# A hybrid attention and MLP layer on one core: 26 identity transposes at the start, and every engine's order drawn anew from refitted durations

## The chip, the cores and the metric

The kernel runs on one core of a Trainium2 chip. Five engines work through lists of their own: TensorE (PE in the profile; its weight loads are PEld), VectorE (DVE), ScalarE (ACT), GpSimd (POOL) and SyncE (SP), which only issues DMAs. An engine takes its list strictly in order; an instruction whose operand is not there holds up all behind it. The metric is the device time of one execution in us, the median of several runs.

## The reference

One layer of a decoder, 1024 tokens of width 1024. Cut to what is computed:

```python
h = rms_norm(x, g_mix_norm)
z = h @ w_in                               # q, 6 x k/v, gates, 3 x conv parts
k_cmp = rms_norm(compress(kc, ...)); v_cmp = compress(vc, ...)   # 63 blocks of 32 tokens, 2-layer MLP
attn_out = nsa_attention(q, k_cmp, v_cmp, k_slc, v_slc, k_win, v_win, gates)
conv_out = short_conv_mixer(hc, cg, bg, conv_w)
mixed = concat(rms_norm(attn_out), rms_norm(conv_out))
x = x + mixed @ w_o
h = rms_norm(x, g_ffn_norm)
x = x + square(relu(h @ w_up)) @ w_down
```

The attention has three branches with a softmax each (compressed blocks, selected blocks, a window of 512 tokens), 8 query heads in 2 groups. All is float32.

## The kernel before

Nearly every product is made of three TensorE sums: both operands are split into a high and a low part (names ending in h and l, hi and lo), and high x high, high x low and low x high are added up in a bank of PSUM, 512 columns wide (`mm3`, `split_psum`, `w_piece`). The stages follow each other and overlap:

- x comes in 8 tiles of 128 tokens. Each is normed (ScalarE squares and sums, GpSimd takes the power, VectorE scales; `norm_in`), transposed on TensorE in 8 pieces of 128x128 (tile `tp` from `xt`) and split (`hTh`, `hTl`). The vectors of the norms, the convolution and the position table arrive as 68 rows (`rows`) and are transposed to `cols`, by which the columns of w_in are scaled on their way in (`w_hi`, `w_lo`).
- The projection z (tiles `zp`) for keys, values, queries and gates. Keys and values of the compressed branch go to DRAM (`kv_d`) and come back in another layout (`ch`), are transposed and go through the compression's two layers (`w1h`, `w1l`, sum `hp`; `compress_steps`).
- The convolution part of z (`zX`, `zZ`, `zW`, with weights `wcr`, `wcuh`, `wcul`), its products `cv`, `MCh`, `MCl`, and the running sums of their squares `sqs` on VectorE. TensorE adds these up over the channels against a column of ones (into a score bank, `s_`). Then the convolution's half of w_o (sums `wc`), while keys come back from DRAM (`kn`) and are transposed (`k_transposes`).
- Attention, block by block of 128 queries: queries are read back (`qx`) and transposed (`tpq`), scores are made in banks `s_`, VectorE adds the distance penalty and takes the minimum of the negated scores (`tensor_tensor_reduce`), ScalarE takes exponentials into `pt` and `pc`, TensorE transposes them (`tp`), they are split into `ph` and `pl` and weigh the values (`ot`). `finish` makes the attention's half of w_o (`wa`).
- The MLP: up-projection and down-projection each with seven products of half-size blocks in place of eight (weights `wu`, `wd`, split as `we`; hidden values through DRAM, `ur`, split as `uu`; banks `X`, `Z`, `W`).

The order of the instructions isn't the order of the code. All operations are recorded as nodes of a graph (`Plan.op`), each with a duration for its engine and a later time at which its result can be used (`Plan.cost`), and a planner lays the graph out on five engines and a line of DMAs (`Plan.schedule`). Where several operations can go, the one with the least slack goes first; the slack of each, its rank, comes from four passes forward and backward (`latest`). Then the ranks are shaken: `shaken` draws, from a seed, a stretch of the plan's time and adds noise to the ranks of what lies in it, and the numbers in SEEDS are applied one after the other (`best`). The emitted lists are the result. `plan.plus` raises or lowers the rank of what is recorded under it; `plan.slack` adds to the planned landing of a DMA. The durations serve the order alone: on the chip each instruction takes what it takes, and waits on semaphores where it depends on another.

The tiles of PSUM that transposes go through come from a ring of three (`psP`, tag `pt`), in the order in which they are recorded.

Of the kernel before, what the change touches and what calls it, by code (L numbers as in the profile page):

```python
# [19 lines left out]
P = 128  # L20
# [61 lines left out]
class View:  # L82
# [33 lines left out]
    def region(self):  # L116
        s = self.shadow
        off = s.__array_interface__["data"][0] - BASE
        key = (off, s.shape, s.strides, self.base.row)
        if key not in REGIONS:  # L120
            pos = np.zeros((1,), np.int64) + off
            for n, st in zip(s.shape, s.strides):
                if st:
                    pos = np.unique((pos[:, None] + np.arange(n) * st).ravel())
            row, col = pos // self.base.row, pos % self.base.row // 4
            bits = np.zeros(self.base.row // 4, np.uint8)
            bits[col] = 1
            REGIONS[key] = int(row.min()), int(row.max()) + 1, int.from_bytes(np.packbits(bits).tobytes(), "big")
        return REGIONS[key]
# [22 lines left out]
SEEDS = (200003, 200016, 200017, 200021, 200023, 200024, 200027, 200038, 200040, 200046, 200057, 200058, 200068, 200073, 200076, 200084, 200110, 200115, 200169, 200182, 200226, 200264, 200290, 200364, 200373, 200407, 200422, 200459, 200470, 200547, 200567, 200605, 200650, 200657, 200676, 200679, 200731, 200752, 200764, 200765, 200783,)  # L152


class Plan:
# [82 lines left out]
    def op(self, name, engine, method, a, kw):  # L238
# [42 lines left out]
        node.plus, node.slack = self.plus, self.slack  # L281
        node.late = node.busy + late
# [7 lines left out]
    plus = 0.0  # L290
    follow = ()
    drag, slack = 1.0, 0.0
    LINK = .05
    GROUP = 1

    def cost(self, name, method, a, kw, views):
# [3 lines left out]
        if method == "dma_start":  # L300
            nb = 4 * max(int(np.prod(v.shadow.shape)) for _, v in views)
            return (.58 if name == "POOL" else .33), 0.0, int(nb * self.drag)
        if name == "PE":
            if method == "transpose":
                c = .109
            else:
                rhs = a[2]
                c = rhs.cols()
                c = max(4 * c / 4560, .218) if rhs.base.args[1] == F32 else max((c if c >= 256 else 4 * c) / 2400 + .014, .109)
            return c, c + .17, 0  # L310
# [7 lines left out]
        if name == "DVE":  # L318
            if method == "tensor_tensor_reduce":
                return .163 + n * .00104, .26 + n * .00104, 0  # L320
# [4 lines left out]
            elif method == "memset":  # L325
                c = .08 + n * .0005
            else:
                c = .064 + n * .00104
            self.port = near and n >= 64
            return c, c + .08, 0  # L330
        self.port = n >= 64
        if method == "tensor_tensor":
            if kw.get("op") == ALU.pow:
                return .4 + .15 * n, .45 + .15 * n, 0
            c = .15 + n * .00213
# [8 lines left out]
    def schedule(self, late=None, weight=lambda n: -.03 * n.k, rings=True):  # L344
# [31 lines left out]
        for n in reversed(topo):  # L376
            own = .4 + n.bytes / .36e6 + 1.75 if n.bytes else n.late
# [20 lines left out]
        while True:  # L398
            while stack:
                n = stack.pop()  # L400
                if n.engine is None:
                    if n.base is not None:
# [4 lines left out]
                        t, last, _, n.users = heapq.heappop(slots[ring])  # L407
                        if t > n.ready:
# [42 lines left out]
            hold = n.hold = .09 * max(0, len(new) - 1)  # L451
# [9 lines left out]
            if n.bytes:  # L461
                line = max(t + .4, line) + n.bytes / .36e6
                done = line + 1.75
# [25 lines left out]
    def latest(self, end):  # L489
# [11 lines left out]
        def settle(n, t):  # L501
            late[n.k] = end - t
            for q in before[n.k]:
                if n.engine is not None and n.engine == q.engine and not q.bytes and (q.engine == "PE" or q.k not in n.raw):
                    r = t
                else:
                    r = t + (self.LINK + .4 + q.bytes / .36e6 + 1.75 - q.busy if q.bytes else
# [49 lines left out]
    def best(self, seeds):  # L557
        end, order = self.schedule()
        found = None
        for _ in range(4):  # L560
            late = self.latest(end)
            end, order = self.schedule(late)
            if found is None or end < found[0]:
                found = end, late, self.starts()
        for seed in seeds:
            late = self.shaken(found[1], found[2], seed)
            found = self.schedule(late)[0], late, self.starts()
        return found
# [14 lines left out]
def trunk_layer(ctx, tc, x, g_mix_norm, w_in, g_q, g_k, pe_cmp, w_cmp1, b_cmp1, w_cmp2, b_cmp2,  # L583
# [118 lines left out]
    with ExitStack() as a:  # L702
# [11 lines left out]
        plan.plus = 0.0  # L714
        tp = psP.tile([P, 512], F32, name="tp", tag="pt")
# [92 lines left out]
    with ExitStack() as b1:  # L808
# [43 lines left out]
        def compress_steps():  # L852
            for kv in range(2):
                yield
                ch = cp.tile([P, 16, HD], F32, name="ch")
                for g in range(G):
                    plan.slack = 2.0
# [127 lines left out]
    with ExitStack() as b2:  # L985
# [313 lines left out]
        for i in range(4):  # L1299
            k_transposes(*kts.pop(0))  # L1300
        wc_done = 0
        for it, tb in [*enumerate(ORDER)][6:] + [*enumerate(ORDER)][:6]:
# [20 lines left out]
            for i in range(2):  # L1323
# [269 lines left out]
    cps_stack.close()  # L1593
    et2 = pool(up_stack, "et2")
# [208 lines left out]
```

## Time and profile before

| | |
|---|---|
| median of 3 runs | 1219.5 us (1219.11 to 1220.33) |
| the profiled execution's own time | 1219.08 us |
| its span, first to last instruction | 1217.3 us |
| TensorE busy | 1197.3 us, 98% |
| VectorE, ScalarE, GpSimd busy | 77%, 59%, 57% |
| DMA | 156 MB, mean 128 GB/s |

The profile shows one execution. A row of the timeline is start, length, engine, line, operation, output and inputs, shapes, how many instructions were merged, and in brackets the idle time before and what ended it. Nearly all instructions have the line L272, the helper that records them, so they are told apart by their tiles. A sum on TensorE is shown with its pipeline's end, so the next one starts before it is over. Queue rows (SPq, ACTq) are issues of DMAs. The chain of waits is followed back from the last instruction; its DMA rows run from issue to landing.

### The profile page before, as it was taken

What the parts mean: (1) busy time and instruction counts of PE and PEld (TensorE: products, weight loads), DVE (VectorE), ACT (ScalarE), POOL (GpSimd) and SP (SyncE); (2) the same over time, 40 slices, a digit from 0 to 9 for tenths busy, and PEclk for the clock granted to TensorE, in tenths of its full rate; (3) what the DMA queues carried; (4) which work ended last, traced back from release to release, by engine and by line L of the source; (5) the groups of instructions that cost most, each with busy time, mean ns of one, the idle gap of its engine ahead of it and who ended that gap; (6) DMA issues with size and microseconds to landing.
All of it is one profiled execution on the core that took longest, in us unless ns stands there. A gap on an engine that the chain in (4) does not pass through costs nothing.

```text
span 1217.3 us, 18290 instructions
## 1 busy us (share of the span) xinstructions
PE 1197.3 (98%) x5970; PEld 997.3 (82%) x5970; DVE 938.2 (77%) x1784; ACT 714.7 (59%) x1586; POOL 695.9 (57%) x629
## 2 busy tenths in 40 slices
PE   7999999999999999999999999999999999999998
PEld 6878977878878888888877888888888888888887
DVE  7947966695697899988977565655658999888985
ACT  7567855562497888787955555555335444344440
POOL 2244410011255545334859877777789998888961
PEclk9999999999999999999999999999999999999999
DMA  7365631165120100002234553535539555543513
GB/s 247 87 182 165 179 83 52 53 208 181 52 71 36 71 1 35 28 18 71 87 121 141 181 183 114 184 110 170 189 134 392 180 167 172 166 156 107 171 44 138
DMA packets 104215, 156.06 MB, mean 128 GB/s; under 512 B 20212, under 2 KB 58184, under 8 KB 104120
## 3 DMA queue, kind: packets, MB, share of 16 engines
q1 hardware_dynamic: 97976, 147.09, 36.9%
q10 hardware_dynamic: 5376, 5.24, 1.3%
q0 software_dynamic: 768, 2.56, 0.7%
q8 instruction: 47, 0.77, 0.3%
q14 instruction: 48, 0.39, 0.1%
HBM read 106.63 MB, written 48.23 MB: 127 GB/s over the span
## 4 chain that ended last, share of the span: by engine, by line
PE 86%; DVE 8%; DMA 3%; ACT 1%; issue 1%; SPq 0%; POOL 0%; ACTq 0%; DVEq 0%; POOLq 0%
PE X L272 27%; PE Z L272 17%; PE tp L272 6%; PE zp L272 6%; PE ot L272 5%; PE zX L272 5%; PE wa L272 4%; PE wc L272 3%; PE W L272 3%; PE zZ L272 2%; PE zW L272 1%; DVE we L272 1%; PE hp L272 1%; DVE y L272 1%; DMA y<-x_d 1%
## 5 line engine op out<-in xcount | busy, mean ns | idle before, releaser
L272 PE MATMUL X<-we,uu 128*128 128x512 f32 x720 | 197.9, 389 | 0.2 <-DVE y L272 0.2
L272 PE MATMUL Z<-we,uu 128*128 128x512 f32 x576 | 164.8, 389 | 0.0
L272 PEld LDWEIGHTS X<-we,uu 128*128 128x128 f32 x720 | 135.0, 188 | 28.7 <-DVE y L272 0.6
L272 ACT ACTIVATE uu<-ur 128x512 fp32r<-128x512 f32 x108 | 67.2, 631 | 133.8 <-PE Z L272 75.5
L272 PEld LDWEIGHTS Z<-we,uu 128*128 128x128 f32 x576 | 108.1, 188 | 22.5
L272 ACT ACTIVATE pt<-pt,nm 128x640 f32<-128x640 f32 (+7 forms) x128 | 93.7, 734 | 39.2 <-DVE nm L272 38.7
L272 DVE TENSOR_TENSOR pl<-tp,ph 128x512 fp32r<-128x512 f32 (+1 forms) x148 | 95.1, 656 | 11.3 <-ACT ph L272 9.7
L272 POOL TENSOR_TENSOR d<-d 128x512 f32<-128x512 f32 x64 | 96.9, 1534 | 10.2 <-DVE d L272 8.1
L272 ACT ACTIVATE ph<-tp 128x512 fp32r<-128x512 f32 (+1 forms) x148 | 82.6, 576 | 26.9 <-PE tp L272 22.6
L272 DVE TENSOR_TENSOR y<-X,y 128x512 f32<-128x512 f32 x128 | 85.4, 683 | 15.9 <-PE X L272 14.4
L272 PE MATMUL tp<-ident,pt 128*128 128x128 f32 x528 | 96.1, 273 | 1.0 <-DVE pl L272 0.4
L272 POOL TENSOR_TENSOR uu<-ur,uu 128x512 fp32r<-128x512 f32 x54 | 85.0, 1577 | 6.0 <-ACT uu L272 5.0
L272 DVE TENSOR_TENSOR we<-s,we 128x512 fp32r<-128x512 f32 x42 | 43.6, 1037 | 48.2 <-ACT we L272 19.8
L272 DVE TENSOR_TENSOR y<-Z,y 128x512 f32<-128x512 f32 x96 | 64.7, 682 | 18.2 <-PE Z L272 18.1
L272 PEld LDWEIGHTS tp<-ident,pt 128*128 128x128 f32 x528 | 67.4, 140 | 12.4 <-issue 0.9
L272 ACT ACTIVATE we<-s 128x512 fp32r<-128x512 f32 x55 | 34.7, 630 | 66.3 <-PE Z L272 38.3
L272 ACT ACTIVATE we<-wu 128x512 fp32r<-128x512 f32 x57 | 35.9, 632 | 51.7 <-PE X L272 37.8
L272 DVE TENSOR_TENSOR uu<-ur,uu 128x512 fp32r<-128x512 f32 x54 | 62.1, 1151 | 3.1 <-PE Z L272 1.4
L272 DVE TENSOR_TENSOR we<-wu,we 128x512 fp32r<-128x512 f32 x38 | 51.9, 1371 | 16.3 <-PE X L272 8.4
L272 POOL IOTA d_sw<- 128x640 f32 (+1 forms) x2 | 1.2, 610 | 109.5 <-PE zZ L272 109.5
L272 PE MATMUL zp<-w_lo,hTh 128*128 128x512 f32 (+1 forms) x192 | 62.7, 362 | 0.0
L272 PE MATMUL zp<-w_hi,hTh 128*128 128x512 f32 (+1 forms) x192 | 62.6, 368 | 0.0
(1334 smaller groups left out, 3710.7 us busy)
## 6 DMA issues: line engine op xcount, KB each, us to landing
u_d<-d SPq DMA_DIRECT2D x112, 256.0 KB, 2.1
ur<-u_d SPq DMA_DIRECT2D x108, 256.0 KB, 2.9
wu<-in_w_up_dram SPq DMA_DIRECT2D x16, 1024.0 KB, 5.9
wd<-in_w_down_dram SPq DMA_DIRECT2D x16, 1024.0 KB, 6.0
xt<-in_x_dram SPq DMA_DIRECT2D x10, 512.0 KB, 4.7
w_raw<-in_w_in_dram SPq DMA_DIRECT2D x8, 512.0 KB, 3.9
w1r<-in_w_cmp_dram SPq DMA_DIRECT2D x16, 256.0 KB, 3.7
q_d<-qn SPq DMA_DIRECT2D x8, 512.0 KB, 4.3
```

The source lines that it names most:

```text
L272: node.do.append(lambda: getattr(engine, method)(*[real(x) for x in a], **{k: real(x) for k, x in kw.items()}))
```

## The change

Six things change together:

- 26 transposes of the identity matrix onto itself, into a tile `warm` that nothing reads, are recorded ahead of the transpose of `rows`, with their rank raised by 200. The planner counts them and nothing else at double duration (`cold`).
- In the stage of w_o's convolution half, four pairs of key transposes were recorded before the first of x's second reads; now the two sums `wc` of the first tile come first, and after it six of the eight pairs.
- A score bank `s_` counts as one piece: whoever touches part of it depends on whoever touched any of it.
- Durations are refitted: DMA issue (.33 to .38, or .58 for some small transfers), DMA latency (1.75 to 1.95 us and a part by size), 512-wide sums (.014 to .0185 of overhead ahead of the last stages, .0135 in them), several operations of VectorE and GpSimd, which of them share a port, the time that several waits cost (`HOLD`, `LOAD`), and the return of a buffer (`BACK`).
- The extra landing time of `ch` goes from 2.0 to 3.5 us.
- SEEDS has 178 numbers, all new, in place of 41.

```diff
     def region(self):
-        s = self.shadow
+        s = self.base.shadow if self.base.kw["name"] == "s_" else self.shadow
...
-SEEDS = (200003, 200016, 200017, ...
+SEEDS = (3000001, 3000010, 3000021, ...
...
+        if self.cold:
+            busy, late = 2 * busy, 2 * late
...
-            return (.58 if name == "POOL" else .33), 0.0, int(nb * self.drag)
+            small = any(v.base.kw["name"] in ("k_d0", "k_d1", "ch") for _, v in views)
+            return (.58 if name == "POOL" or small else .38), 0.0, int(nb * self.drag)
...
-                c = max(4 * c / 4560, .218) if rhs.base.args[1] == F32 else max((c if c >= 256 else 4 * c) / 2400 + .014, .109)
+                c = max(4 * c / 4560, .218) if rhs.base.args[1] == F32 else max((c if c >= 256 else 4 * c) / 2400 + (self.SLOW if c == 512 else .014), .109)
...
-            hold = n.hold = .09 * max(0, len(new) - 1)
+            n.extra = len(new) - 1
+            hold = n.hold = max(0.0, n.ready + self.HOLD * n.extra - t)
+            if n.bytes:
+                hold = n.hold = max(hold, self.HOLD * (n.extra + 1))
+            elif e == "PE" and n.cause is not None and nodes[n.cause].engine != "PE":
+                hold = n.hold = max(hold, n.ready + self.LOAD - t)
...
                 line = max(t + .4, line) + n.bytes / .36e6
-                done = line + 1.75
+                done = line + 1.95 + n.bytes * .7e-6
...
+        tp = psP.tile([P, 512], F32, name="warm", tag="pt")
+        plan.plus, plan.cold = 200.0, True
+        for _ in range(26):
+            nc.tensor.transpose(tp[:, :P], ident, ident)
+        plan.plus, plan.cold = 0.0, False
...
-                    plan.slack = 2.0
+                    plan.slack = 3.5
...
-        for i in range(4):
-            k_transposes(*kts.pop(0))
...
-            for i in range(2):
+            for i in range(6 if len(kts) == 8 else 2):
                 if kts:
                     k_transposes(*kts.pop(0))
...
+    plan.SLOW = .0135
```

No operation but the 26 transposes is added or taken away. What moves is the order, everywhere on every engine. Three places, before and after:

TensorE from its first instruction: the transposes of x's tiles (`xt`), of `rows`, and the first sums of the projection (`zp`). Before:

```order
L272 MATMUL tp<-ident,xt 128x128 x4
L272 MATMUL tp<-ident,rows 128x68
L272 MATMUL tp<-ident,xt 128x128 x12
L272 MATMUL zp<-w_hi,hTh_172 128x512 x2
L272 MATMUL tp<-ident,xt 128x128 x4
L272 MATMUL zp<-w_lo,hTh_172 128x512
L272 MATMUL zp<-w_hi,hTl_171 128x512
```

Now:

```order
L272 MATMUL warm<-ident 128x128 x26
L272 MATMUL tp<-ident,rows 128x68
L272 MATMUL tp<-ident,xt 128x128 x15
L272 MATMUL zp<-w_hi,hTh_172 128x512
L272 MATMUL tp<-ident,xt 128x128
L272 MATMUL zp<-w_hi,hTh_172 128x512
L272 MATMUL zp<-w_lo,hTh_172 128x512 x2
```

The transpose of `rows` now stands ahead of all of x, and four transposes that stood between the first sums and the low part's have moved behind.

SyncE where the compression's input `ch` is read back, behind the loads of the compression's weights (`w1r`, and the small `w_895`, which is `w_922` in the new program). Before:

```order
L272 DMA w1r<-in_w_cmp_dram 128x2x256 x2
L272 DMA w_895<-in_w_cmp_dram 128x2x64
L272 DMA w_raw<-in_w_in_dram 128x2x280
L272 DMA v_ds<-vrow 128x256 x2
L272 DMA k_d_193<-krow 256x1x64 x2
L272 DMA w1r<-in_w_cmp_dram 128x2x256
L272 DMA ch<-kv_d 64x1024 x2
```

Now:

```order
L272 DMA w1r<-in_w_cmp_dram 128x2x256 x2
L272 DMA w_922<-in_w_cmp_dram 128x2x64
L272 DMA ch<-kv_d 64x1024 x2
L272 DMA w_raw<-in_w_in_dram 128x2x280
L272 DMA v_ds<-vrow 128x256
L272 DMA k_d_193<-krow 256x1x64
```

The two reads of `ch` have moved ahead of six other issues.

VectorE at the end of the convolution, around the last two running sums of squares (`sqs`, one for each half of the tokens; `hTl` is w_o's scaled low part, `KL` the low part of transposed keys). Before:

```order
L272 TENSOR_TENSOR sqs_2165<-sqs_2165,cv 128x512
L272 SCALAR_TENSOR_TENSOR hTl_171<-wor,cols,hTh_172 128x512
L272 TENSOR_TENSOR MCl<-cv,MCh 128x512
L272 SCALAR_TENSOR_TENSOR hTl_171<-wor,cols,hTh_172 128x512
L272 TENSOR_TENSOR KL<-tp,KH_3029 64x512
L272 TENSOR_TENSOR sqs_2164<-sqs_2164,cv 128x512
```

Now:

```order
L272 TENSOR_TENSOR cv<-cv,c_2917 128x512
L272 TENSOR_TENSOR MCl<-cv,MCh 128x512 x2
L272 TENSOR_TENSOR sqs_2195<-sqs_2195,cv 128x512
L272 TENSOR_TENSOR KL<-tpk,KH_3060 64x64
L272 TENSOR_TENSOR KL<-tpk,KH_3061 64x64
L272 TENSOR_TENSOR sqs_2194<-sqs_2194,cv 128x512
```

Four tasks of full width have left the place between the two sums, and two small ones have come. On TensorE, 12 sums `wc`, the transpose `tpk` and 8 key transposes stood between the convolution's last product and the first product of these sums with the ones; now 22 sums `wc` and `tpk` stand there.

More of the change, by code (lines that the diff above doesn't have):

```diff
@@ L289 @@
     last_pe = None
-    plus = 0.0
+    plus, cold = 0.0, False
     follow = ()
@@ L293 @@
     LINK = .05
+    HOLD = .06
+    BACK = .06
+    LOAD = .1
+    SLOW = .0185
     GROUP = 1
@@ L318, in cost @@
         if name == "DVE":
+            self.port = near and n > 1 and (method in ("tensor_tensor", "scalar_tensor_tensor", "tensor_copy")
+                                            or method == "tensor_scalar" and n != 12)
             if method == "tensor_tensor_reduce":
-                return .163 + n * .00104, .26 + n * .00104, 0
+                self.port = False
+                c = .079 + n * .00104 + .06 * isinstance(kw.get("scalar"), View)
+                return c, c + .13, 0
             if method == "scalar_tensor_tensor":
@@ L326, in cost @@
                 c = .08 + n * .0005
+            elif method == "reciprocal":
+                return .14, .3, 0
             else:
                 c = .064 + n * .00104
-            self.port = near and n >= 64
             return c, c + .08, 0
@@ L334, in cost @@
                 return .4 + .15 * n, .45 + .15 * n, 0
-            c = .15 + n * .00213
+            wide = any(0 in v.shadow.strides for _, v in views)
+            c = .143 + n * .00167 if wide else .15 + n * .00213
             return c, c + .05, 0
@@ L376, in schedule @@
         for n in reversed(topo):
-            own = .4 + n.bytes / .36e6 + 1.75 if n.bytes else n.late
+            own = .4 + n.bytes / .29e6 + 1.95 if n.bytes else n.late
             n.prio = own + max([s.prio for s in n.succ + more[n.k]], default=0.0)
@@ L407, in schedule @@
                         t, last, _, n.users = heapq.heappop(slots[ring])
+                        t += self.BACK * (n.users != {})
                         if t > n.ready:
@@ L506, in settle @@
                 else:
-                    r = t + (self.LINK + .4 + q.bytes / .36e6 + 1.75 - q.busy if q.bytes else
+                    r = t + (self.LINK + .4 + q.bytes / .29e6 + 1.95 - q.busy if q.bytes else
                              self.LINK * (n.engine is not None) + max(0.0, q.late - q.busy))
@@ L564, in best @@
                 found = end, late, self.starts()
+        late = found[1]
         for seed in seeds:
-            late = self.shaken(found[1], found[2], seed)
-            found = self.schedule(late)[0], late, self.starts()
-        return found
+            late = self.shaken(late, found[2], seed)
+        return (self.schedule(late)[0], late, self.starts()) if seeds else found
     def issue(self):
```

2 lines of the change are left out of this document (1 added, 1 removed).

## The prediction, made before the result was known

> **What bounds the kernel now.** I read the page's head first, then the table of busy time by stage, then the waits of TensorE (PE).
>
> ```profile
> span 1217.3 us, 18290 instructions
> PE 1197.3 (98%) x5970; PEld 997.3 (82%) x5970; DVE 938.2 (77%) x1784; ACT 714.7 (59%) x1586; POOL 695.9 (57%) x629
> 7.30:11.00 3.70, 3.48 (x16) 3.11 (x17) 2.31 (x6) 2.77 (x6) 1.10 (x2) 1.00 0.95 290
> 320.00:400.00 80.00, 77.47 (x477) 64.72 (x476) 68.94 (x239) 67.74 (x177) 40.91 (x71) 1.00 0.20 67
> 400.00:500.00 100.00, 99.97 (x632) 87.46 (x631) 90.89 (x328) 81.82 (x184) 45.88 (x73) 1.00 0.08 30
> 500.00:610.00 110.00, 109.63 (x675) 93.61 (x674) 97.30 (x242) 92.03 (x189) 58.49 (x64) 1.00 0.15 53
> 650.00:920.00 270.00, 269.78 (x1188) 222.30 (x1187) 166.52 (x164) 138.80 (x262) 214.78 (x148) 1.00 0.48 163
> ```
>
> The last five rows are stretches in us: length, then busy time and count of PE, weight loads, VectorE, ScalarE and GpSimd, then granted clock, DMA share and GB/s. PE is busy nearly everywhere, and the number of its sums is the same after the change but for the 26 added transposes, so only time in which PE stands still, or runs slowly, can be won. In the up-projection (650 to 920) there is almost none of it; it lies in the head, in scattered waits, and in the attention stage's first part. What ended PE's waits:
>
> ```profile
> PE tp L272 <- DVE rs_t L272: 7.3, 1, 7.3
> PE tp L272 <- DMA ch<-kv_d: 1.4, 1, 1.4
> PE hp L272 <- ACT w1h L272: 1.1, 1, 1.1
> PE s__3049 L272 <- DVE sqs L272: 1.0, 1, 1.0
> PE tpq L272 <- DMA qx<-q_d: 0.7, 1, 0.7
> PE zX L272 <- ACT wcuh L272: 0.6, 1, 0.6
> ...
> ```
>
> The columns are total us, times, longest. The view has 17 rows and 18 waits, 15.5 us in all; the last row is one wait of 0.2. Without the head of 7.3 that is 8.2 us in 17 waits. Each wait costs a little more than it shows, because the modelled end of a sum lies beyond the start of the next:
>
> ```profile
> 1205.06 8.10 PE L272 MATMUL Z<-we,uu 128*128 128x512 f32 x35
> 1204.83 0.39 PE L272 MATMUL X<-we,uu 128*128 128x512 f32 x1
> ```
>
> 35 sums in a row take 8.10, so one follows the other every (8.10 - 0.39) / 34 = 0.227 us while each is shown with 0.39; a wait hides 0.16. The 17 waits then cost 8.2 + 17 x 0.16 = 10.9 us. This is what a better order can win, beside the slow start below.
>
> **The change, part by part.** All engines' lists are drawn anew. I follow three places through them and estimate the rest.
>
> *The start.* The 26 transposes need only the identity, so they can run before x arrives.
>
> ```profile
> 1.04 0.29 POOL L272 TENSOR_SCALAR_AFFINE_SELECT ident<-ident 128x128 f32<-128x128 f32 x1
> 7.31 1.11 PE L272 MATMUL tp<-ident,xt 128*128 128x128 f32 x4 [7.31 <-DVE rs_t L272]
> 8.61 0.58 ACT L272 ACTIVATE hTh<-tp 128x512 fp32r<-128x512 f32 x1
> 8.63 0.34 PE L272 MATMUL tp<-ident,rows 68*128 68x68 f32 x1 [0.21 <-DMA rows<-in_g_out_dram]
> 8.77 2.76 PE L272 MATMUL tp<-ident,xt 128*128 128x128 f32 x12
> 10.36 0.71 ACT L272 ACTIVATE w_hi<-w_raw,cols 128x512 fp32r<-128x512 f32 x1
> 11.19 1.22 PE L272 MATMUL zp<-w_hi,hTh 128*128 128x512 f32 x2
> 13.27 0.40 PE L272 MATMUL zp<-w_hi,hTl 128*128 128x512 f32 x1
> 18.97 1.03 PE L272 MATMUL tp<-ident,xt 128*128 128x128 f32 x8
> L272 PE MATMUL tp<-ident,xt 128*128 128x128 f32 x20 | 4.9, 417 | 7.3 <-DVE rs_t L272 7.3
> 3.67 4.83 DMA rows<-in_g_out_dram
> ```
>
> The last row but one is the group of the first 20 transposes, 7.0 to 13.2 us: mean 417 ns. In the row of 8 at 18.97 one follows another every (1.03 - 0.27) / 7 = 0.109 us, in the row of 12 at 8.77 every (2.76 - 0.42) / 11 = 0.213. So PE runs at half rate from 7.31 to about 13, although the granted clock of 7.30 to 11.00 reads 1.00 above. The 26 at 0.213 last 5.5 us, from 1.35 to about 6.9: before anything else is ready, and as long as the slow stretch itself, 5.7 us. If they bring the full rate forward, 20 transposes save 20 x 0.104 = 2.1 and the three 512-wide sums about 0.5: a gain of at most 2.6. Against it stands the new list: the transpose of rows is now PE's first after the 26, ahead of x, and rows land at 3.67 + 4.83 = 8.50. The first copy by ScalarE moves from 8.61 to 8.50 + 0.14 + 4 x 0.11 + 0.17 = 9.25, that is 0.65 later, the loss if nothing catches up. ScalarE then does hTh, hTh, w_hi without the pause that it had after 8.61 (second copy only at 9.86, for PE was slow), and w_hi begins near 10.3 as before. So the first 512-wide sum starts at 11.1 either way; only what PE did from 11.19 to 13.27 shrinks: three sums and four transposes, 3 x 0.23 + 4 x 0.11 = 1.13 us of 2.08. Part of these 0.95 goes to waits for ScalarE and VectorE: I take **-0.7**, within -2.6 and +0.65.
>
> Those rows speak on a rule of the Trainium skill, TensorE: Matmul & The Clock Gate, "Part 4: PE-mode transpose": the full rate does not engage for transposes, which do not count as busy in the same way. By it the 26 would warm nothing, the term would be nearer +0.65, and the sum 1.35 higher. Here full rate came at 13, some 2 us after the first sum, with 20 transposes before it; that rather speaks for transposes counting, but no run shown has transposes alone.
>
> *The compression's input.* Transposes of ch wait for a DMA that SyncE issues late.
>
> ```profile
> 65.89 0.42 ACTq L272 DMA_DIRECT2D kv_d<-z  x1
> 67.85 0.37 SPq L272 DMA_DIRECT2D w<-in_w_cmp_dram  x1
> 73.11 0.39 SPq L272 DMA_DIRECT2D w1r<-in_w_cmp_dram  x1
> 74.05 1.15 SPq L272 DMA_DIRECT2D ch<-kv_d  x2
> 74.60 5.04 DMA ch<-kv_d
> 77.73 0.63 PE L272 MATMUL zp<-w_lo,hTh 128*128 128x512 f32 x2
> 79.78 0.63 PE L272 MATMUL tp<-ident,ch 128*128 128x128 f32 x4 [1.41 <-DMA ch<-kv_d]
> kv_d<-z ACTq DMA_DIRECT2D x8, 128.0 KB, 2.1
> ```
>
> Its source was whole at 65.89 + 2.1 = 68.0, but six issues stood between w (67.85) and ch (74.05): a weight load, two of v, two of k, one of w1r. In the new list ch stands right behind w, so it goes out near 68.5, the second at 69.1, and lands by 74.1. The first ch transpose stands 65.3 us of PE work into the list where it stood 66.7 before (sums and transposes ahead of it by the durations above), so PE comes to it at about 78.2 - 1.4 - 0.7 = 76.1: two us to spare. The other six issues move behind ch by its 1.15 us, with nothing on PE waiting. The wait was 1.41 + 0.16: **-1.6**, and 0 if kv_d's last part comes 2 us later.
>
> *Sums of squares of the convolution.* PE waits for VectorE's running sum.
>
> ```profile
> 266.92 0.39 PE L272 MATMUL zX<-t4h,wcul 128*128 128x512 f32 x1
> 270.74 1.25 DVE L272 TENSOR_TENSOR sqs<-sqs,cv 128x512 f32<-128x512 f32 x1
> 272.05 0.61 PE L272 MATMUL s__3049<-ones,sqs 128*128 128x1 f32 x4 [1.01 <-DVE sqs L272]
> 274.56 0.67 DVE L272 TENSOR_TENSOR sqs<-sqs,cv 128x512 f32<-128x512 f32 x1
> ```
>
> The first sum is ready 5.1 us after the last product of the convolution starts (266.92 to 272.05). Between them PE had 12 sums of w_o, 9 transposes: 12 x 0.227 + 9 x 0.109 = 3.7, and its own 0.23. Now it has 22 sums and one transpose, 5.1 + 0.23: no wait. The second running sum came 8.3 us after that product (275.23), with four other tasks between the two on VectorE; now only two small ones stand there, so I put it at 5.1 + 0.4 + 0.7 = 6.2, while PE asks at 5.8. Of the 1.01 + 0.16 = 1.17 lost, 0.4 comes back: **-0.8**; -1.2 if none, +1.3 if the second is as late as before (8.3 - 5.8 - 1.17).
>
> *All else.* 5.8 us of listed waits in 15 places are left, 5.8 + 15 x 0.16 = 8.2 with what they hide. Their order is redrawn by a list of durations that the trace can judge. For 256 KB on SyncE the kernel's list gave 0.40 + 0.73 + 1.75 = 2.88 us to landing and now, by the diff, 0.40 + 0.73 + 1.95 + 0.18 = 3.26:
>
> ```profile
> 376.42 3.53 DMA qx<-q_d
> ```
>
> For ch, with its own allowance of 2.0 and now 3.5, it gave 4.88 and now gives 6.76, where the row shows 5.04. So both DMA waits of the view were planned too short, and that error shrinks or turns. A 512-wide sum was 0.2273 and becomes 0.2318, where 35 in a row show 0.227: worse. I expect some old waits to go and some new ones to come, and take a third off, as two of the 17 waits, and the longer ones, are what I could follow to an end: **-2.7**, from -8.2 (all gone) to the +8.7 of the second rival. Before the trace of the change nobody can add these up place by place.
>
> Sum: -0.7 - 1.6 - 0.8 - 2.7 = -5.8. The profiled execution took 1219.1 (span 1217.3 and 1.8 around it), so it becomes 1213.3. The median shown is 0.4 higher, 1219.5: **1213.7 us**. The end of the program, from the row of 35 sums on, has the same order on all engines, so it gives nothing.
>
> **The rivals.**
>
> *Waits are conserved.* PE takes its list in order, so what it gains at ch and at the sums of squares it may spend at the next operand that is late: the third and sixth rows of the waits (w1h, wcuh) end at ScalarE, which no part of the change makes faster. For it: 17 waits of at most 1.4 us, all at different places. Against it: the stretch 400 to 500 shows that an order with 0.03 us idle exists. If the three named gains are given back, the time is 1219.5, within 1217.1 and 1222.
>
> *VectorE becomes the bound of the attention stage* (slower). The list now treats a score bank as one piece: a minimum over part of it is planned behind all products of that bank. VectorE, 90.89 of 100 us busy at 400 to 500, would get its work later and bunched, and ScalarE's exponentials and PE's transposes of them would follow. Price: 320 to 400 shows such a stretch, 2.53 us idle in 80. If all 290 us were like it, 9.2 idle instead of 2.93: +6.3, and at about 0.4 us a wait 16 more waits hide 16 x 0.16 = 2.5: +8.7. With the named -3.1: 1225. It decides from 2.4 us over 1219.5 on, so from 5.5 us of new loss. Against it: the products of one bank stand side by side already.
>
> *Nearly all goes.* All listed waits vanish and the start gives its 0.7: 1219.5 - 10.9 - 0.7 = 1207.9. For it: each wait has its own operand, and none needs more than some 2 us of other work in between. Against it: no list of durations is right to a tenth of a us.
>
> *The 26 do not warm.* Half rate until 13 as before, with rows first: +0.65 in place of -0.7, so 1213.7 + 1.35 = 1215.0. The rule quoted above from the Trainium skill, TensorE: Matmul & The Clock Gate, is this mechanism.
>
> **How the numbers follow.** Forecast 0.50 (1209.5 to 1216.5), nearly all goes 0.17, the 26 do not warm 0.08, conserved 0.15, VectorE 0.10. A measurement of this kernel tells 0.2%, 2.4 us, from no change. The first three cases are faster: 0.75; conserved is the same: 0.15; VectorE slower: 0.10. The range leaves out most of the last and the far end of the second: 1206 to 1221.
>
> **What would show it.** A group of 26 transposes on tile warm that ends before 7.5 us, and then a mean near 273 instead of 417 ns for the transposes of x; if that mean stays near 417, they did not warm. No PE wait for ch, with its issue before 70 us; no wait of 0.5 us or more for sqs. Listed PE waits of about 4 us outside the head instead of 8.2, and 1.3 us or less in 320 to 400. I am wrong if the waits list is as long as now with other names, or if 400 to 610 shows more than 3 us idle with VectorE above 95%.

## The result, and the profile after

The changed kernel took **1207.9 us** (median of 4, 1207.08 to 1208.31) beside 1219.9 for the kernel before (1219.11 to 1221.73): a ratio of 0.990, 95% interval 0.9886 to 0.9918. On a second occasion it took 1211.7 (1208.93 to 1212.18) beside 1218.4, ratio 0.9939 (0.9924 to 0.9954). It is faster in both, by 12 and by 6.7 us; what separates the two is taken up at the end. The profiled execution took 1207.57.

The page's head of the changed kernel, its table by stage with the columns known from above, and its waits of TensorE, all of them:

```profile
span 1205.8 us, 18347 instructions
PE 1196.5 (99%) x5996; PEld 1001.9 (83%) x5996; DVE 925.4 (77%) x1784; ACT 711.2 (59%) x1586; POOL 707.8 (59%) x629
320.00:400.00 80.00, 78.82 (x509) 68.88 (x508) 71.62 (x275) 70.96 (x196) 43.03 (x77) 1.00 0.20 70
400.00:500.00 100.00, 100.00 (x639) 88.12 (x639) 90.87 (x315) 82.68 (x174) 47.28 (x69) 1.00 0.09 30
500.00:610.00 110.00, 109.54 (x662) 92.71 (x661) 95.90 (x218) 87.82 (x181) 61.35 (x60) 1.00 0.14 49
PE warm L272 <- POOL ident L272: 1.4, 1, 1.4
PE tp L272 <- DMA rows<-in_g_ffn_norm_dram: 1.3, 1, 1.3
PE tpq L272 <- DMA qx<-q_d: 1.0, 1, 1.0
PE tp L272 <- DVE t L272: 0.5, 1, 0.5
PE X L272 <- DVE y L272: 0.3, 2, 0.2
PE tp L272 <- DVE hTl L272: 0.2, 1, 0.2
```

The first two waits and the last belong to the start. Outside it 1.8 us in 4 waits are left of 8.2 in 17 (one of the 17, 0.2 for `rows`, was at the start). VectorE is as busy as before at 400 to 500 (90.87 of 100), and TensorE (PE) never stops there.

The start, first by groups (busy time, mean ns of one, idle time before), then in order of time:

```profile
L272 PE MATMUL warm<-ident 128*128 128x128 f32 x26 | 5.8, 423 | 1.4 <-POOL ident L272 1.4
L272 PE MATMUL tp<-ident,xt 128*128 128x128 f32 x20 | 3.1, 278 | 0.3 <-DVE hTl L272 0.2
8.45 0.25 PE L272 MATMUL tp<-ident,rows 68*128 68x68 f32 x1 [1.27 <-DMA rows<-in_g_ffn_norm_dram]
9.18 1.09 ACT L272 ACTIVATE hTh<-tp 128x512 fp32r<-128x512 f32 x2 [0.71 <-PE tp L272]
10.15 0.72 ACT L272 ACTIVATE w_hi<-w_raw,cols 128x512 fp32r<-128x512 f32 x1
10.92 0.50 PE L272 MATMUL zp<-w_hi,hTh 128*128 128x512 f32 x1
```

The 20 transposes of x run at 278 ns in place of 417, after nothing but transposes. The issue of `ch`; then the convolution's last product, the sums of squares on TensorE and the second running sum on VectorE; and last, TensorE's row for that second sum in the kernel before:

```profile
68.49 1.16 SPq L272 DMA_DIRECT2D ch<-kv_d  x2
262.63 0.39 PE L272 MATMUL zZ<-hTh,wcul 128*128 128x512 f32 x1
268.01 2.06 PE L272 MATMUL s__3079<-ones,sqs 128*128 128x1 f32 x16
268.29 0.67 DVE L272 TENSOR_TENSOR sqs<-sqs,cv 128x512 f32<-128x512 f32 x1
```
```profile
275.43 0.95 PE L272 MATMUL s__3049<-ones,sqs 128*128 128x1 f32 x8
```

To see where the time went, I give each TensorE instruction of a trace the spacing that it has when nothing holds it up (0.227 us for a 512-wide sum, 0.109 for a transpose of 128), and add these up along the list, without the 26. That is the work ahead of an instruction; the lists of all kernels have the same 1178 us of it. The table says how much later each kernel starts the instruction with so much work ahead of it than the changed kernel of the first profile does. Each column is one profiled execution, and the second occasion (e5) shows that it moves: by a few tenths, and by 1.4 at the end.

| work ahead, us | before | e1 | e2 | e3 | e4 | e5 | e9 |
|---|---|---|---|---|---|---|---|
| 20 | 0.55 | 1.17 | -0.33 | -0.57 | 0.28 | 0.70 | 0.69 |
| 66 | 0.41 | 1.19 | -0.47 | -0.58 | 1.19 | 0.69 | 0.56 |
| 70 | 2.11 | 1.19 | 1.42 | -0.58 | 1.18 | 0.69 | 2.95 |
| 120 | 3.89 | 2.32 | 3.26 | -0.58 | 1.16 | 0.68 | 3.26 |
| 245 | 4.51 | 2.37 | 4.64 | -0.79 | 0.99 | 0.79 | 3.16 |
| 270 | 5.85 | 2.36 | 5.98 | -0.81 | 0.97 | 0.74 | 3.57 |
| 320 | 7.43 | 2.32 | 7.61 | -0.82 | 1.22 | 0.72 | 3.63 |
| 340 | 7.03 | 1.39 | 8.39 | -0.30 | 0.34 | 1.22 | 4.66 |
| 380 | 9.62 | 1.36 | 10.53 | -0.35 | 0.29 | 1.26 | 5.78 |
| 640 | 11.98 | 1.23 | 12.72 | -0.33 | 0.18 | 1.15 | 6.39 |
| 1177 | 11.47 | 1.15 | 12.10 | 0.59 | 0.42 | 1.38 | 6.22 |

Read down the column of the kernel before: 0.55 of the gain is made at the start, 1.70 at `ch` (66 to 70), 1.34 at the sums of squares (245 to 270), and the other 7.9 in between and behind: 1.8 from 70 to 120, 0.6 from 120 to 245, 3.8 from 270 to 380, 2.4 from 380 to 640, less 0.5 given back in the down-projection and 0.1 before 66.

### The profile page after: what moved, and what is told of

Its sections match the earlier page's. It is cut to its first block, busy times and chain, and to the rows that moved or that the text cites. A ratio compares the mean times of both kernels' runs of the same rounds, so it can differ in the third digit from the quotient of the medians.

```text
span 1205.8 us, 18347 instructions
## 1 busy us (share of the span) xinstructions
PE 1196.5 (99%) x5996; PEld 1001.9 (83%) x5996; DVE 925.4 (77%) x1784; ACT 711.2 (59%) x1586; POOL 707.8 (59%) x629
## 4 chain that ended last, share of the span: by engine, by line
PE 90%; DVE 5%; issue 2%; ACT 1%; DMA 1%; POOL 0%; SPq 0%; DVEq 0%; ACTq 0%; POOLq 0%
PE X L272 28%; PE Z L272 16%; PE zp L272 8%; PE tp L272 6%; PE ot L272 5%; PE zX L272 5%; PE wa L272 4%; PE wc L272 4%; PE W L272 3%; PE zZ L272 3%; PE zW L272 1%; DVE y L272 1%; PE hp L272 1%; DVE uu L272 1%; DVE we L272 1%
## 5 line engine op out<-in xcount | busy, mean ns | idle before, releaser
L272 PE MATMUL tp<-ident,pt 128*128 128x128 f32 x528 | 93.2, 272 | 0.0
L272 POOL MEMSET Qz<- 64x512 f32 x16 | 8.3, 520 | 119.1 <-PE zZ L272 107.8
L272 DVE TENSOR_TENSOR uu<-ur,uu 128x512 fp32r<-128x512 f32 x54 | 65.6, 1217 | 2.9 <-ACT uu L272 1.3
L272 PE MATMUL zp<-w_hi,hTl 128*128 128x512 f32 (+1 forms) x192 | 64.9, 364 | 0.0
L272 POOL TENSOR_TENSOR we<-wd,we 128x512 fp32r<-128x512 f32 x32 | 47.4, 1483 | 26.1 <-ACT we L272 24.4
```

The source lines that it names most:

```text
L272: node.do.append(lambda: getattr(engine, method)(*[real(x) for x in a], **{k: real(x) for k, x in kw.items()}))
```

## The experiments

My theory was that most of the gain comes from the refitted durations, by which the planner's lists stall seldom; that the 26 transposes bring the full rate forward and are worth well under 1 us; and that the early issue of `ch` is worth its 1.6 us. The rivals: the 26 do nothing or are nearly all of it; later waits give back what a place gains; the greater number of draws, not the durations, made the order.

### The 26 transposes

e1 is the changed kernel with its lists on all engines, less the 26:

```diff
+        node.cold = self.cold
...
             for n in order:
+                if n.engine == "PE" and n.cold:
+                    continue
                 for f in n.do:
```

> The changed kernel's lists on all engines, without the 26 transposes of the identity. Theory (the 26 bring the full rate forward): the first 20 transposes of x go back from a mean of 278 ns to about 417, the first sum of the projection (10.9 us in the changed kernel) comes at most 0.5 us later because ScalarE and the rows set it, and the four sums and transposes behind it run at half rate; at the sum numbered by 20 us of TensorE work it is 0.7 to 1.2 us behind the changed kernel, 1207.9 becomes 1208.6 to 1209.1. Rival (they warm nothing, the transposes of x do it themselves): the mean stays near 278 and the time within 0.3 us of 1207.9. Second rival (the warm start is most of the whole gain): 1212 or more.

e2 is the kernel before, with its lists, and the 26 put ahead of TensorE's first instruction:

```diff
+            first = next(n for n in order if n.engine == "PE")
             for n in order:
+                if n is first:
+                    o, i = [v.real() for v in self.heat]
+                    for _ in range(26):
+                        self.tc.nc.tensor.transpose(o, i, i)
...
+        plan.heat = tp[:, :P], ident
```

> The kernel before, all lists as they were, with the 26 transposes of the identity put ahead of TensorE's first instruction. Theory: the transposes of x, first at 7.3 us as before, run at a mean near 278 ns in place of 417, the first 512-wide sum comes at about 10.5 to 11.0 instead of 11.19 and the time falls by 0.8 to 1.8 us, 1219.5 to 1218 or so: the warm start is worth about a tenth of what the change won. Rival (the warm start is what the change won): 1212 or less. Rival (transposes don't bring the full rate): mean 417, time within 0.4 us of the kernel before.

The transposes of x in the first 14 us, by groups, first of e1, then of e2:

```profile
L272 PE MATMUL tp<-ident,xt 128*128 128x128 f32 x17 | 4.1, 412 | 0.0
```
```profile
L272 PE MATMUL tp<-ident,xt 128*128 128x128 f32 x24 | 3.8, 280 | 0.2
```

Without the 26 the half rate is back (412 ns), with them it is gone in the old list too (280). So transposes alone bring the full rate. At 20 us of work e1 is 1.17 behind, as expected, and e2 0.88 ahead of the kernel before (-0.33 against 0.55). In the whole little is left: e1 took 1208.4 us (1208.16 to 1208.72, where I had put 1208.6 to 1209.1) at a ratio of 0.9920 (0.9905 to 0.9935), which cannot be told from the changed kernel's, though its profiled execution still ends 1.15 behind. e2 took 1218.1 beside 1218.2, ratio 0.9996 (0.9987 to 1.0006): its 0.88 is gone at 245 us of work, spent on a wait of 1.6 for `wcuh` where the kernel before waited 0.6. My 0.8 to 1.8 for e2 did not come; the 26 in front of the old list win nothing that can be measured.

### Where the start and ch are worth less than they look

e3 moves the transpose of rows, and VectorE's copy of it, behind the first 8 of x; e4 moves the first two reads of ch behind the six issues that stood ahead of them before. Both change only where these nodes stand in the emitted order (`move`, not shown, takes the picked ones out and puts them in behind another):

```diff
+        x = [n for n in named if n.names == "transpose tp xt ident"]
+        picks = [n for n in named if n.names in ("transpose tp rows ident", "tensor_copy cols tp")]
+        order = self.move(order, picks, x[7])
```
```diff
+        ch = [n for n in sp if n.names == "dma_start ch kv_d"][:2]
+        w1 = [n for n in sp if n.names.startswith("dma_start w1r")][2]
+        order = self.move(order, ch, w1)
```

> The changed kernel, with one transpose moved: that of rows (and VectorE's copy of it) stands behind the first eight transposes of x, not ahead of them. In the changed kernel TensorE is idle from 7.2 us, when the 26 are over, to 8.45, when rows land, while x can be transposed from about 7.3. Theory: the copies hTh and with them w_hi come 0.7 to 1.0 us earlier, the first sum at 10.0 to 10.3 in place of 10.9, and the time falls by 0.5 to 0.9 us, if no later wait gives it back. Rival (later waits, on DMA and VectorE, give it back): within 0.2 us of 1207.9.

> The changed kernel, with SyncE's two reads of ch put back behind the six issues that stood ahead of them before; nothing else is moved. Theory (this place is worth the 1.6 us that the prediction gave it, and no later wait hides it): ch is issued near 74 us, TensorE waits 2.5 to 4 us for it since it now comes to that place earlier (76.3) than before (78.2), and the time rises by 2 to 4 us, to 1210 to 1212. Rival (waits are conserved, the lists have room behind it): TensorE waits at ch, but at 120 us of TensorE work the delay is below 0.5 us, and the time within 0.7 us of 1207.9.

e3 took 1208.2 us (1208.09 to 1208.42), ratio 0.9918 (0.9904 to 0.9933), not the 0.5 to 0.9 less that I had put. Its first sum came at 9.96, and at 20 us of work it led by 0.57, as expected. It kept the lead to 320, lost 0.5 of it at 340 and 0.9 more between 640 and the end, most of that in one wait of 0.6 for `y`. e4 took 1207.4 (1206.91 to 1207.99), ratio 0.9912 (0.9897 to 0.9927), no slower than any other form of the change. It did wait for ch, though 0.7 and not 2.5 to 4, for ch went out at 72.2 and not near 74:

```profile
PE tp L272 <- DMA ch<-kv_d: 0.7, 1, 0.7
```

It lost 0.9 there (66 us of work), still had that at 120, where the rival had put less than 0.5, and had it back at 340. One transfer stands at that place. Rows of the changed kernel, then the same in e3, then in e4:

```profile
341.46 0.63 PE L272 MATMUL tpq<-ident,qx 128*128 128x128 f32 x4
342.12 4.10 DMA qx<-q_d
346.35 0.30 PE L272 MATMUL tpq<-ident,qx 128*128 128x128 f32 x1 [0.96 <-DMA qx<-q_d]
```
```profile
340.64 0.63 PE L272 MATMUL tpq<-ident,qx 128*128 128x128 f32 x4
341.30 4.63 DMA qx<-q_d
346.07 0.30 PE L272 MATMUL tpq<-ident,qx 128*128 128x128 f32 x1 [1.51 <-DMA qx<-q_d]
```
```profile
342.69 0.63 PE L272 MATMUL tpq<-ident,qx 128*128 128x128 f32 x4
343.35 0.33 SPq L272 DMA_DIRECT2D qx<-q_d  x1
346.45 0.27 PE L272 MATMUL tpq<-ident,qx 128*128 128x128 f32 x1
```

There is one buffer for `qx`, so its next read goes out only when the transposes of the last one are over: 0.66 us after the first of them in all three. The read moves with TensorE, then, and what TensorE has won ahead of it is not lost by that. What differs is how long the transfer takes: 4.10 us in the changed kernel, 4.63 in e3 and 4.61 in e5, where TensorE waits 0.96, 1.51 and 1.49; in e4 and e1 TensorE goes on 3.1 us after the issue and does not wait. e3's loss and e4's gain at 340 are this transfer's length, and why it differs no run shows. So e4 does not show that waits are conserved. It shows that the early ch is worth 0.9 at its place in the changed kernel (the 1.70 of the table is what the whole new order won there), and that this is no more than single transfers move further on: by the medians, 1207.4 and 1207.9, nothing of it can be measured.

### Durations or draws

e7 and e8 are both kernels with nothing drawn (`SEEDS = ()`), e5 the changed kernel unaltered beside them. e9 is the changed kernel with the first 41 of its 178 numbers, as many as the kernel before has; e10 the kernel before with 35 more numbers taken by its own durations.

> The changed kernel once more, unaltered, as the measure beside the next three, and a second look at the start, for in one of the runs with the same first instructions the 26 transposes took 4.9 us and in others 5.4 and 5.8. Theory (TensorE's rate is decided at moments that have no fixed place in the program, some 3.4 us apart, by how busy it was): the spacing changes from 213 to 109 ns at some other instruction than before, 5 to 7.5 us into the span, and the time is 1207 to 1208.5. Rival (the change comes after a fixed number of instructions): it comes at the same place as in the first profile, between the 26th and the rows.

> The kernel before, with no number in SEEDS: the planner's ranks as the four passes make them, nothing drawn. Theory (the durations decide how well the plan holds on the chip; the draws refine it): 1222 to 1232, with 25 or more waits of TensorE. Rival (the draws make the order, the durations matter little): the same time as the changed kernel without draws, within 2 us.

> The changed kernel with no number in SEEDS. Theory (durations): already without draws it is 4 to 12 us below the kernel before without draws, at 1212 to 1220, because the list's waits are where the chip has them; the draws bring the rest. Rival (the longer search is what won, 178 numbers in place of 41): within 2 us of the kernel before without draws.

> The changed kernel with the first 41 of its 178 numbers in SEEDS, as many as the kernel before has. Theory (the refitted durations carry the gain): 4 to 8 us below the kernel before in the same call, TensorE's listed waits outside the start under 4.5 us. Rival (the number of draws carries it): within 2.4 us of the kernel before.

> The kernel before with 35 more numbers in SEEDS, 76 in place of 41, drawn and taken by its own, old durations; else unaltered. Theory (durations): the old list takes its waits for short where the chip has them long, so more draws by it move the time by less than 2.4 us either way, and the waits of 0.5 us and more are as many as before, in other places. Rival (draws): 4 us or more below the kernel before.

e11 and e12 put a part of the old durations back, in e11 the cost of waits, in e12 that of DMAs:

```diff
-    BACK = .06
+    BACK = 0.0
...
-            hold = n.hold = max(0.0, n.ready + self.HOLD * n.extra - t)
...
+            hold = n.hold = .09 * max(0, n.extra)
```
```diff
-            return (.58 if name == "POOL" or small else .38), 0.0, int(nb * self.drag)
+            return (.58 if name == "POOL" else .33), 0.0, int(nb * self.drag)
...
-                done = line + 1.95 + n.bytes * .7e-6
+                done = line + 1.75
...
-                    plan.slack = 3.5
+                    plan.slack = 2.0
```

e12 also puts the old latency and rate into the ranks (`latest`) and takes the cost of several waits off the issue of a DMA.

> The changed kernel with the old cost of waits (0.09 us for each wait beyond the first, nothing for a weight load behind another engine or for a returned buffer), and SEEDS drawn anew for it from the first 756 numbers, as for the kernel with 41, of which it takes 23. All else is the change's. Theory A (what a wait costs is the part of the refit that matters): 3 us or more above the kernel with 41 numbers, with waits of TensorE on VectorE and ScalarE back. Theory B (the DMA durations matter): within 1.5 us of the kernel with 41 numbers.

> The changed kernel with the old durations of DMAs (issue 0.33, flight 1.75 us and 0.36 MB per us, 2.0 us extra for ch), and SEEDS drawn anew from the first 756 numbers, of which it takes 49. All else is the change's. Theory A: within 1.5 us of the kernel with 41 numbers; a wait for ch or qx of 1 to 1.6 us may return. Theory B: 3 us or more above it, with waits of TensorE for DMA of 2.5 us or more in sum outside the start.

Medians in us, with the ratio to the kernel before and its interval, each taken beside it:

| | nothing drawn | 41 numbers, or as many tries | more |
|---|---|---|---|
| old durations | 1225.0, 1.0054 (1.0037 to 1.0071) | 1218.2 to 1219.9, 1 | 76 numbers: 1221.1, 1.0016 (1.0001 to 1.0031) |
| refitted | 1219.2, 1.0004 (0.9995 to 1.0013) | 1213.7, 0.9949 (0.9932 to 0.9965) | 178 numbers: 1207.9, 0.9902; again 1211.7, 0.9939 |
| refitted, old cost of waits | | 1216.4, 0.9972 (0.9957 to 0.9986) | |
| refitted, old DMAs | | 1217.2, 0.9982 (0.9972 to 0.9993) | |

At equal draws the change (durations, the score bank as one piece, the recorded order and the 26 together; no run takes the second or the third back alone) is worth 5.8 us without any and 5.2 with 41. Draws are worth 6.6 by the old durations, and then no more: 35 further ones, each of which shortens the plan, left the kernel no faster (+2.2), as I had put it, with 7 waits of half a us and more outside the start in place of 6. By the refitted ones 41 bring 0.0055 of 1218 by the ratios, 6.7 us, and the other 137 bring 1.2 us (0.9949 to 0.9939) or 5.7 (to 0.9902), by the occasion. e7 and e8 lie where I had put them, e7 with 17 listed waits in place of 25. e5's time missed my 1207 to 1208.5.

The 5.8 is not spread over the list. By the measure of the table above, e7 is 2.5 us ahead of e8 at 245 us of work. From there to 270 e7 falls back by 6.9, e8 by 2.3. TensorE's longest wait of e7 there, and the stretch around it with its granted clock:

```profile
269.30 1.09 PE L272 MATMUL tp<-ident,kn 128*128 128x128 f32 x4 [3.94 <-issue]
267.80:274.50 6.70, 5.20 (x15) 4.26 (x16) 6.06 (x11) 1.86 (x3) 0.00 (x0) 0.50 1.08 357
```

What the wait of 3.94 us was for the profile does not say. The rate fell to half within it, at 267.7, for 6.8 us; TensorE was busy for 5.2 of these, so some 2.6 us were lost, an estimate. All four executions of e7 have a mean granted clock of 0.997, where e8's ten have 0.999 to 1.000. So some 2.6 of the 5.8, and of the 6.6, go with one fall of the rate, and the wait ahead of it is more than all the rest of the 5.8.

Either half of the refit taken back costs 2.7 (e11) or 3.6 (e12) of the 5.2 by the medians, just short of theory A's 3 for e11, and as theory B had it for e12. But each is one order out of one search, and e10 shows that other draws alone move 2.2. And much of both goes with falls of the rate too: e9's four executions have a mean granted clock of 0.999 or 1.000, three of e11's five have 0.997 or 0.998, and nine of e12's ten 0.996 to 0.998. The other two of e11 took 1214.1 and 1215.0, the other one of e12 1215.2, that is 0.5 to 1.5 above e9's median. That the halves matter apart from such falls is not shown. The waits on transfers outside the start that theory B named did come in e12; e9 has none of them, but one as long on ScalarE. First e12, then e9:

```profile
PE tp L272 <- DMA ch<-kv_d: 2.4, 1, 2.4
PE tpq L272 <- DMA qx<-q_d: 1.5, 3, 0.7
```
```profile
PE hp L272 <- ACT ah L272: 2.0, 1, 2.0
```

At 120 us of work e12 is 3.0 behind the changed kernel and e9 3.3, so the wait for ch is not what makes e12 the slower. In the profiled executions e12 ends 1.8 behind e9, and 1.6 of that arises between 245 and 270 us of work, where its rate falls.

For the cost of waits the listed sums do not tell, being like e9's (about 5 us in both; I had expected under 4.5 for e9). What e11 lost most by is the next point.

### A fall of the clock behind a short wait

TensorE's rows of e11 at the sums of squares, and two stretches of its table by stage:

```profile
270.95 1.95 PE L272 MATMUL s__3090<-ones,sqs 128*128 128x1 f32 x16 [0.52 <-DVE sqs L272]
275.94 1.05 PE L272 MATMUL wc<-hTh,MCl 128*128 128x512 f32 x2
278.01 0.62 PE L272 MATMUL wc<-hTh,MCl 128*128 128x512 f32 x2
270.00:273.00 3.00, 2.48 (x19) 2.06 (x19) 0.76 (x2) 0.17 (x1) 0.00 (x0) 1.00 1.09 348
273.00:276.50 3.50, 3.50 (x12) 2.69 (x12) 0.55 (x3) 0.34 (x2) 1.64 (x1) 0.64 0.89 303
```

A wait of half a us and 16 products of a single column, 1.95 us, and then the granted clock is 0.64 over 3.5 us and two sums take 1.05 in place of 0.62. e12 shows the same in its rows at this place, and so does e10, with a wait of 0.58 for `KL` and four transposes ahead of the 16. The kernel before and e2 (wait 1.01, but 4 products ahead of the rest) do not, in the executions profiled, nor do the changed kernel, e1, e3 to e6, e8 and e9 (16 products, no listed wait right ahead of them). That the wait and the narrow products together bring the fall is how I read these rows; no run alters this place alone. Between 245 and 270 us of work e11 fell back 3.6 us on the changed kernel, some 2.1 of it here and the rest in two later waits for `y`; e9 fell back 0.4.

At the start one sees the same clock. In e4 the 26 ended early, rows came late, and the rate fell again:

```profile
1.38 4.93 PE L272 MATMUL warm<-ident 128*128 128x128 f32 x26 [1.38 <-POOL ident L272]
8.25 0.25 PE L272 MATMUL tp<-ident,rows 68*128 68x68 f32 x1 [1.94 <-DMA rows<-in_g_ffn_norm_dram]
9.00:12.00 3.00, 3.00 (x15) 2.51 (x13) 2.60 (x6) 2.64 (x5) 0.55 (x1) 0.50 1.00 326
```

By the starts of its instructions the spacing went from 213 to 109 ns at 5.3, back to 213 at 8.7, and to the full rate by 12.3 us: turns 3.4 and at most 3.6 us apart. The trace's own record of the granted clock has these turns at 5.27, 8.68 and 12.10, and the stretches between turns that it has in other traces (6.83 and 256.00 us in e7, 597.33 in e6, 1198.08 in the changed kernel) are whole multiples of 3.413 us. In the changed kernel's first profile all 26 ran at 213; in e3, e5 and e6 the turn came at 6.1, 5.7 and 7.4, so it is not bound to a fixed instruction, as e5's rival had it. This is what the Trainium skill, TensorE: Matmul & The Clock Gate, "Part 1: The HAM clock gate (the "warmup" mystery)" states: activity is judged in free-running windows of about 3.4 us, so the moment changes from run to run. The traces agree. Its rule of thumb in the section "HAM oscillation — how this bites in real kernels", no idle gaps above some 3.4 us, is too lenient for e4, where 2.1 us of idle time (1.94 listed) went ahead of the fall; e5, with 1.8 listed, kept the rate. e11's 0.5 us ahead of narrow products would be a second case, if the reading above holds.

e6 was to keep TensorE busy until rows land, with 40 in place of 26:

```diff
+        node.cold = self.cold
...
+            last = [n for n in order if n.engine == "PE" and n.cold][-1]
             for n in order:
-                for f in n.do:
+                for f in n.do * (15 if n is last else 1):
```

> The changed kernel with 40 in place of 26 transposes of the identity, so that TensorE is busy until 7.7 to 8.8 us, when rows land. Theory (the full rate is lost again when TensorE stands idle between the 26 and rows, as it did in one run after 2 us of idle time): the transposes of x run at a mean near 278 ns, TensorE's idle time ahead of rows is below 0.8 us, the spacing goes from 213 to 109 ns within the row and not back; the time is 0 to 0.6 us below the unaltered changed kernel of the same call. Rival (the loss in that run had another cause, such as the transpose of rows): the mean is 350 or more again, or the time 0.5 us or more above.

It took 1212.5 us (1209.28 to 1214.62) beside e5's 1211.7, where I had put 0 to 0.6 below; ratio 0.9948 (0.9930 to 0.9966): no gain, and the 0.8 above is within the spread. The start did as expected (turn within the row, no fall, 0.3 behind the first profile at 20 us of work), but the profiled execution, at 1214.62, shows something else. VectorE, GpSimd and TensorE there, then VectorE's same operation in e5:

```profile
597.48 1.30 POOL L272 TENSOR_TENSOR s<-wu 128x512 f32<-128x512 f32 x1
597.85 4.92 DVE L272 TENSOR_SCALAR xn<-ylast,rffn 128x512 f32<-128x512 f32 x1
598.75 1.29 POOL L272 TENSOR_TENSOR wu<-wu 128x512 f32<-128x512 f32 x1
600.00 1.26 POOL L272 TENSOR_TENSOR wu<-wu,s 128x512 f32<-128x512 f32 x1
601.23 1.25 POOL L272 TENSOR_TENSOR wu<-wu 128x512 f32<-128x512 f32 x1
603.43 0.66 PE L272 MATMUL tp<-ident,y 128*128 128x128 f32 x4 [2.71 <-DVE T4l L272]
604.00:609.00 5.00, 5.00 (x20) 3.91 (x20) 3.45 (x6) 1.67 (x3) 3.06 (x3) 0.66 0.01 3
```
```profile
595.92 1.17 DVE L272 TENSOR_SCALAR xn<-ylast,rffn 128x512 f32<-128x512 f32 x1
597.61 0.92 DVE L272 TENSOR_SCALAR xn<-ylast,rffn 128x512 f32<-128x512 f32 x1
```

The operation began 0.37 us after the first of four GpSimd instructions and ended 0.29 after the last; elsewhere it takes about 1. TensorE waited 2.71 us for what stood behind it on VectorE, and then had the half rate for 3.4 us: 3.9 us lost in one place. The plan lets operations of the two engines that share a port take turns (`port` in `Plan.schedule`), but it has no wait through four of them and no fall of the rate. Another 2.8 us was lost between 80 and 120 us of work, for the most part around short waits for `w1h`, `w1l` and `hx` that the first profile of the same list does not have; why, no run shows.

## Why the prediction was right, and where its size was off

The forecast was 1213.7 with 1206 to 1221, and faster; 1207.9 and 1211.7 lie inside. The forecast gain of 5.8 was about half of the first measured one; that the second lies near 1213.7 is luck in part, for its executions seem to hold falls of the clock (below) that no term of the sum had. By its steps:

- **The start**, -0.7: 0.55 in the first profile, at 20 us of work. Its parts came where they were put: rows at 8.45 (8.50), the first copy at 9.18 (9.25), the first sum at 10.92 (11.1). The last of the 26 started at 6.8, since none reached the full rate in that execution. On the second occasion (e5) it is 0.15 behind the kernel before there (0.70 against 0.55), with a wait of 0.4 for `w_hi` that the first profile does not have. By e1 the 26 are worth 1.17 at 20 us of work, and the rest of the new start costs 0.62, near the 0.65 of the sum. In the medians at the end the warm start cannot be measured (e1, e2).
- **The 26 do not warm** (the rule of the Trainium skill, TensorE: Matmul & The Clock Gate, "Part 4: PE-mode transpose"): refuted, 278 ns against 412 without them.
- **ch**, -1.6: 1.70 where it stood; issue at 68.49 (68.5), TensorE there at 76.3 (76.1), no wait. That it also lasts to the end was not said but meant, and no run shows it: e4 lost 0.9 there and had it back by the length of another transfer.
- **Sums of squares**, -0.8: 1.34, near the bound without any wait (-1.2). The second running sum came 6.3 us after the last product's start (6.2), as put; wrong was that 4 products stand ahead of the first that needs it. By the row of 8 in the kernel before it is 8 of the 16, so TensorE asks at 6.3 too and not at 5.8, and nothing waits.
- **All else**, -2.7 within -8.2 and +8.7: this is the term that was mis-sized, 7.9 in the first profile. I took a third off 15 waits that I had not followed; 4 of the 15 are left or have new names. Listed time fell from 5.8 to 1.8, 11 waits fewer hide 11 x 0.16 = 1.8, and some 2 us more were in gaps too short to be listed, which my sum did not have. What I held against the rival "nearly all goes", that no list of durations is right to a tenth of a us, seems not to count: as I read it, the list need only be right to what each operand has in hand. That rival's 1207.9 is the first result, by luck in part: 1.8 us of listed waits stayed, and the 2 us of short gaps were not in its sum either.
- **VectorE as the bound**: refuted, 0.5 us idle from 400 to 610, and VectorE at 91% and 87%.
- **Waits are conserved**: wrong for the whole. For single small gains it is not decided: e2's 0.88 was gone at 245 us of work and e3's 0.57 at the end, but part of e3's went, and e4's loss came back, by the length of one transfer.

Of the signs that I named, the 26 end at 7.2 (before 7.5), 320 to 400 is idle 1.18 (at most 1.3), no wait for sqs is 0.5, and the listed waits outside the head are 1.8, not about 4.

What stays open: why the changed kernel's executions of the second occasion spread from 1208.93 (the one profiled, mean granted clock 1.000) to 1212.18 (three at 0.996 to 0.998). A mean of 0.997 over 1210 us at a rate of one half would be 0.003 x 1210 / 0.5 = 7 us at half rate, some 3.6 us lost, an estimate from these figures; it would fit one or two falls like those of e11 or e6, but none of those three executions was traced. e1 to e4 ran on one chip (the three forms of the change at 1207.4 to 1208.4), e5 to e8 on a second and e9 to e12 on a third, so whether the chip has a part in the falls is not told either. Open too is which part of the change, and how much of it by way of the clock, makes the 5 us at equal draws.

## What to carry to other kernels

Where an order comes from a planner, fit its durations and waits to the trace before searching longer: at equal draws the change with its refit won 5 us here, while nearly twice the draws by the old durations won nothing. Before you credit a part of a change with a few us, see whether they are spread over the list or sit in one stall or one fall of the clock (3.9 us in e6, 6.9 in e7); and undo each part singly, against the half us that one transfer's length moves. Suspect a wait of TensorE in front of narrow work of costing more than its length.

## What the runs showed of the hardware that I had not expected

- Transposes alone bring TensorE to full rate, 2.9 (e9) to 6.1 us (e6) after the first of them, and the granted clock in the profile reads 1.00 through that first half rate, but 0.50 when the rate falls later (e4).
- Half a us of waiting and 16 single-column products stood ahead of a fall to half rate for 3.41 us in all three profiles that have both (e10, e11, e12); none of the eight with the 16 and no wait right ahead shows one.
- The same read of 256 KB at the same place took 4.10 us in one execution and 4.61 and 4.63 in others.
- One VectorE operation on 128x512, `xn`, stretched over four GpSimd instructions in a row (4.92 us in place of about 1.0) in one execution. The Trainium skill, SBUF — State Buffer, "Who interferes with whom", states that a pair of ports to that memory is shared by the two engines, and that, against a VectorE operation in a mode that uses both of its ports (`tensor_scalar` can), the one which gets the pair holds it for a whole instruction while the other blocks. The rows agree with blocking, though none shows the mode; that an operation can be passed over several times in a row, as they suggest, it does not say.
